# Where the running maximum lives, who masks the diagonal score blocks, and when the summing transfers leave: one change to a hybrid attention block on one Trainium2 core

## The chip, the cores and the metric

The program runs on one core of one Trainium2 chip. A core has five engines that run their own instruction streams in order and wait for each other on semaphores: TensorE (PE in the profile, with its weight loads on a second row, PEld), VectorE (DVE), ScalarE (ACT), GpSimd (POOL) and SyncE (SP), which only issues transfers. GpSimd issues some transfers too, those that add into DRAM. The metric is the device time of the program in microseconds, as a median of runs.

## The reference

The reference is a decoder block on a sequence of 1040 tokens (16 learned meta tokens before 1024 real ones) with 1024 channels. One RMS norm and one input projection feed two mixers: a causal multi-scale pooling and a forgetting attention with 8 heads of 64. Both are gated, projected up, merged with sigmoid gates, projected once more and added to the residual. Cut to the attention, which the change touches most:

```python
c = cumsum(log_sigmoid(f_logit + b_forget), axis=1)
s = einsum('bqhd,bkhd->bhqk', qb, kb) / sqrt(64)
s = s + c[:, :, q0:q1, None] - c[:, :, None, :q1]
s = where(valid, s, -inf)            # causal
p = softmax(s, axis=-1)
o = einsum('bhqk,bkhd->bqhd', p, vb)
y_attn = o * silu(z_attn)
```

## The kernel before, in words

All products run in fp32 accuracy by splitting each operand in a high part (float32r) and a low part, so that a product is three matmul groups: high by high, high by low, low by high. `whi`/`wlo`, `ph`/`pl`, `yh`/`yl`, `gw`, `gh` are such pairs. ScalarE makes the high parts, and VectorE or GpSimd subtract them from the source for the low parts.

The program has four stages: the norm and the first projections; the scores with softmax, among which the other projections are strewn; the block products that make the gates' inputs (seven products `g_prod` per result, Strassen's way); the up-projections and the last product, again by seven block products.

The score stage has 16 units: 4 head pairs `p`, 2 heads `e`, 2 halves of 512 queries. Scores stand transposed: keys on the 128 partitions, queries along the row. A unit of the first half has 5 key blocks, one of the second half 9. For a key block `b`, `Unit.qk` runs two matmuls into a PSUM bank `ps` (pool `psS`, two banks), and the result goes to SBUF as `S` with a per-key bias `negc` (the running sum of the forget gates). Where the block lies on the diagonal, its first up to 128 columns need the causal mask; `d1` is where the masked columns end and `c0` where the block begins. Before, VectorE evicted the masked columns with bias and mask in one instruction (L687), and ScalarE evicted the rest (L689), into the same tile. Then VectorE brought the running maximum `m`, an SBUF tile, up to date (L693 to L696). After the last block `Unit.maxes` reduces `m` over the keys: a 32x32 block transpose, a reduction, and two exchanges between partition groups by small ScalarE copies; the result is spread into a PSUM bank `pm`. `Unit.soft` then, block by block, subtracts `pm` (L720, VectorE), takes the exponential (L721, ScalarE), copies the high part `ph` (L724, ScalarE), subtracts for the low part `pl` (L725, VectorE), adds up the sums in `acc` (L731 and L733, GpSimd) and, two blocks later, multiplies by the values into `po` (L741). `Unit.finish` takes `po` out (L748) and stores it in two parts, `y` and `y2`, that a GpSimd transfer adds in DRAM (`add_y`).

`merged` strings the key blocks of the next unit and the softmax steps of this one together, and `F.pull` puts matmuls of other projections (`g_proj`, L170) between them. For TensorE the order in the program is the order of execution (`manual_schedule`), and the pull lengths are fixed numbers. On the other engines a scheduler of the framework orders the instructions by its own estimates; `after` ties an instruction to stand behind another in that order without a wait, `behind` makes it wait for the other's end.

`SUMS` lists what each unit does on the side: stores and loads of blocks for the later products (`put`, on SyncE), negated blocks (`put_neg`: a ScalarE copy, two GpSimd subtractions, stores) and transfers that add one DRAM block to another (`add`, on GpSimd). They were issued after `u.finish()`, and ordered behind the last sum `accs[-1]`.

The PSUM pool `psT` has two banks and serves `pm` and, near the end, one result each of the groups `ga_` and `gb_`. At the end of the gates' stage, four pooling products `pool_mm` (L170 on `plh`, `pll`) alternate with the seventh product on the four results `ga_[0]` to `ga_[3]`; each result must have been added to `zp` (`plus_`, L982) before its next product may begin. `up_weights` loads and splits the weights of an up-projection (L1098, L1099).

Of the kernel before, what the change touches and what calls it, by code (L numbers as in the profile page):

```python
# [54 lines left out]
def tile_hybrid_block(ctx, tc, x, meta, norm_g, w_in, b_forget, pool_w, pool_scale,  # L55
# [560 lines left out]
    def add_y(p):  # L616
        d, r = [spill[n, p].rearrange("(p k) c -> p (k c)", k=2) for n in ("y", "y2")]
        after(nc.gpsimd.dma_start(d, r, accum_op=ALU.add, max_dma_last_dim=8192), accs[-1])
# [26 lines left out]
    class Unit:  # L645
# [19 lines left out]
        def qk(self, b):  # L665
            p, e, q0, t0, kb, c0 = self.p, self.e, self.q0, self.t0, self.kb[b], self.c0[b]
            h = 2 * p + e
            ka, qa, ql = KA[p, e], QA[p, e], QL[p, e]
            d1 = max(0, min(512, b * KB + KB - t0))
            own_keys = b == NB - 1  # L670
            if b == 0:
                self.m = ap_.tile([KB, 512], F32, name="m")
            m = self.m
            if b % 2 == 0:
                self.st = ap_.tile([KB, 2, 512], F32, name="S", tag="s", bufs=6)
            s = self.st[:, b % 2, :]
            self.S.append(s)
            ps = psS.tile([128, 512], F32, name="ps")
            k0 = KS[b]
            nc.tensor.matmul(ps[:kb, c0:], ka[:, k0:k0 + kb], qa[:, q0 + c0:q0 + 512], start=True, stop=False)  # L680
            nc.tensor.matmul(ps[:kb, c0:], ka[:, k0:k0 + kb], ql[:, q0 + c0:q0 + 512], start=False, stop=True)  # L681
            nb_ = negc[:kb, b, h:h + 1]
            f0 = max(d1, c0)
            if d1 > c0:
                j = t0 + c0 - b * KB
                mk = tail if own_keys else mask[:, j:j + d1 - c0]
                nc.vector.scalar_tensor_tensor(s[:kb, c0:d1], ps[:kb, c0:d1], nb_, mk, op0=ALU.add, op1=ALU.add)  # L687
            if f0 < 512:
                nc.scalar.activation(s[:kb, f0:], ps[:kb, f0:], AF.Identity, bias=nb_)  # L689
            S0 = self.S[0]  # L690
            if b == 1:
                if c0:
                    nc.vector.tensor_copy(m[:, :c0], S0[:, :c0])  # L693
                nc.vector.tensor_tensor(m[:, c0:], S0[:, c0:], s[:, c0:], op=ALU.max)
            elif b > 1:
                nc.vector.tensor_tensor(m[:kb, c0:], m[:kb, c0:], s[:kb, c0:], op=ALU.max)  # L696

        def maxes(self, extra=0.0):
# [45 lines left out]
        def finish(self):  # L744
# [3 lines left out]
            nc.scalar.activation(t, po, AF.Copy)  # L748
            for n, part in (("y", hr), ("y2", lr)):
# [246 lines left out]
    add_y(3)  # L996
# [350 lines left out]
```

## Time and profile before

| | |
|---|---|
| median of 3 runs | 745.23 us (744.98 to 746.96) |
| the profiled execution's own time | 744.3 us |
| its span from first to last instruction | 742.6 us |
| TensorE busy | 720.2 us (97%) |
| VectorE, ScalarE, GpSimd busy | 536.5, 417.0, 334.4 us |
| mean granted TensorE clock | 0.996 |

An engine is busy while an instruction of it runs. Groups of instructions are named by line, engine, operation, output<-input and the shapes; after the bar stand their busy time, the mean of one in ns, the idle time of the engine just before them, and what ended it. A row of waits reads: engine, tile and line that waited, the engine and line that ended the wait, microseconds in total, times, longest. PEclk is the clock that TensorE was granted, as a share of full speed.

### The profile page before, as it was taken

How to read it: one execution, taken by the hardware profiler on the slowest of the kernel's cores; microseconds unless marked ns; L12 is line 12 of the kernel's file. 1: busy time of each engine (PE TensorE's matmuls, PEld its weight loads, DVE VectorE, ACT ScalarE, POOL GpSimd, SP SyncE). 2: the span in 40 equal slices, each digit the busy share in tenths (PEclk: the TensorE clock that was granted, in tenths of full speed). 3: DMA queues.
4: the chain of work that ended last, by engine and by line, in shares of the span. 5: the costliest groups of instructions: out<-in, count | busy, mean ns of one | idle time of the engine just before them, and what ended most of it. 6: DMA issues, size and time to landing. Idle time of an engine off the chain costs nothing.

```text
span 742.6 us, 10841 instructions
## 1 busy us (share of the span) xinstructions
PE 720.2 (97%) x3637; PEld 616.6 (83%) x3637; DVE 536.5 (72%) x917; ACT 417.0 (56%) x914; POOL 334.4 (45%) x410
## 2 busy tenths in 40 slices
PE   8999999999999899999999999999989999999996
PEld 6997989997888797898988878888868888888885
DVE  4743577777889687887877858875876554887775
ACT  6752567565675666576765566342764432626445
POOL 4412245658336584365543766473843001005243
PEclk9999999999999999999999999999999999999999
DMA  9301125897864975738475586495905457672006
GB/s 285 77 26 32 29 67 194 206 330 170 221 194 92 237 202 161 192 68 208 124 173 120 134 214 229 117 342 174 307 16 170 143 184 258 222 266 76 0 1 227
DMA packets 88906, 120.45 MB, mean 162 GB/s; under 512 B 11377, under 2 KB 54385, under 8 KB 86786
## 3 DMA queue, kind: packets, MB, share of 16 engines
q1 hardware_dynamic: 85216, 100.36, 43.0%
q0 software_dynamic: 2336, 16.78, 12.2%
q10 hardware_dynamic: 1298, 2.63, 0.9%
q8 instruction: 28, 0.46, 0.3%
q14 instruction: 28, 0.23, 0.1%
HBM read 93.33 MB, written 54.72 MB: 199 GB/s over the span
## 4 chain that ended last, share of the span: by engine, by line
PE 71%; DVE 9%; ACT 8%; issue 4%; DMA 1%; POOL 0%; POOLq 0%; DVEq 0%; ACTq 0%; SPq 0%
PE pj L170 45%; PE pj L1227 8%; PE pj L967 6%; PE po L741 4%; PE pt L1227 2%; DVE pl L725 2%; PE pt L967 2%; PE ps L680 2%; ACT S L689 2%; PE ps L681 2%; ACT S L721 1%; ACT ph L724 1%; PE pj L515 1%; DVE m L696 1%; ACT whi L156 1%
## 5 line engine op out<-in xcount | busy, mean ns | idle before, releaser
L170 PE MATMUL pj<-hh,whi 128*128 128x512 f32 (+3 forms) x640 | 145.6, 354 | 0.0
L170 PE MATMUL pj<-hh,wlo 128*128 128x512 f32 (+3 forms) x640 | 143.6, 351 | 0.0
L170 PE MATMUL pj<-hl,whi 128*128 128x512 f32 (+3 forms) x640 | 142.7, 352 | 0.0
L158 POOL TENSOR_TENSOR wlo<-raw,whi 128x256 fp32r<-128x256 f32 x116 | 91.7, 871 | 97.9 <-ACT whi L156 41.5
L170 PEld LDWEIGHTS pj<-hl,whi 128*128 128x128 f32 x640 | 108.9, 190 | 12.0
L170 PEld LDWEIGHTS pj<-hh,whi 128*128 128x128 f32 x640 | 108.8, 190 | 11.8
L170 PEld LDWEIGHTS pj<-hh,wlo 128*128 128x128 f32 x640 | 108.6, 190 | 11.5
L725 DVE TENSOR_TENSOR pl<-S,ph 128x512 fp32r<-128x512 f32 (+4 forms) x112 | 89.3, 811 | 21.2 <-ACT ph L724 20.8
L733 POOL TENSOR_TENSOR acc<-acc,S 128x272 f32<-128x272 f32 (+4 forms) x80 | 76.7, 959 | 12.5 <-ACT S L721 6.6
L689 ACT ACTIVATE S<-ps,negc 128x400 f32<-128x400 f32 (+2 forms) x96 | 48.7, 515 | 47.9 <-DVE S L687 44.4
L696 DVE TENSOR_TENSOR m<-m,S 128x272 f32<-128x272 f32 (+4 forms) x80 | 47.6, 595 | 21.1 <-ACT S L689 18.9
L721 ACT ACTIVATE S<-S 128x512 f32<-128x512 f32 (+4 forms) x112 | 49.3, 478 | 17.2 <-DVE S L720 17.0
L724 ACT ACTIVATE ph<-S 128x512 fp32r<-128x512 f32 (+4 forms) x112 | 52.3, 479 | 7.2 <-PE po L741 6.9
L136 POOL TENSOR_TENSOR gw<-graw,gw 128x256 fp32r<-128x256 f32 x40 | 44.3, 1187 | 23.5 <-ACT gw L947 14.6
L720 DVE TENSOR_TENSOR S<-S,pt 128x512 f32<-128x512 f32 (+4 forms) x112 | 50.7, 498 | 0.6
L967 PE MATMUL pj<-gh,gw 128*128 128x512 f32 x180 | 43.7, 400 | 2.6 <-DVE zp L982 2.6
L680 PE MATMUL ps<-qa,ka 128*128 128x512 f32 (+4 forms) x112 | 37.6, 335 | 7.7 <-ACT S L689 7.5
L1120 DVE TENSOR_TENSOR rl<-pj,rl 128x512 f32<-128x512 f32 x32 | 22.0, 690 | 30.3 <-PE pj L170 30.2
L967 PEld LDWEIGHTS pj<-gh,gw 128*128 128x128 f32 x180 | 34.9, 194 | 10.5 <-issue 3.0
L156 ACT ACTIVATE whi<-raw 128x512 fp32r<-128x512 f32 x58 | 33.9, 622 | 12.6 <-PE pj L170 6.2
L741 PE MATMUL po<-pl,V 128*128 128x512 f32 (+4 forms) x112 | 38.1, 340 | 2.9 <-DVE pl L725 2.6
L731 POOL TENSOR_TENSOR acc<-S 128x400 f32<-128x400 f32 (+1 forms) x16 | 20.0, 1250 | 41.5 <-ACT S L721 41.4
(228 smaller groups left out, 1345.1 us busy)
## 6 DMA issues: line engine op xcount, KB each, us to landing
raw<-in_w_in_dram SPq DMA_DIRECT2D x31, 512.0 KB, 5.9
gs<-in_w_in_dram SPq DMA_DIRECT2D x5, 1024.0 KB, 6.9
td<-in_w_out_dram SPq DMA_DIRECT2D x5, 1024.0 KB, 10.6
xt<-in_x_dram SPq DMA_DIRECT2D x8, 512.0 KB, 7.8
sp_y<-t SPq DMA_DIRECT2D x32, 128.0 KB, 2.6
gs<-gs POOLq DMA_DIRECT2D x4, 1024.0 KB, 8.7
sp_gp<-st SPq DMA_DIRECT2D x16, 256.0 KB, 4.7
td<-td POOLq DMA_DIRECT2D x4, 1024.0 KB, 8.4
```

What stands on the lines that cost most here:

```text
L158: ins = nc.gpsimd.tensor_tensor(lo[:, k:k + 2], raw[:, k:k + 2], r32(hi[:, k:k + 2]), op=ALU.subtract)
L170: nc.tensor.matmul(ps, a, b, start=(i == 0), stop=(i == len(seq) - 1))
L680: nc.tensor.matmul(ps[:kb, c0:], ka[:, k0:k0 + kb], qa[:, q0 + c0:q0 + 512], start=True, stop=False)
L689: nc.scalar.activation(s[:kb, f0:], ps[:kb, f0:], AF.Identity, bias=nb_)
L696: nc.vector.tensor_tensor(m[:kb, c0:], m[:kb, c0:], s[:kb, c0:], op=ALU.max)
L721: exps.append(nc.scalar.activation(s[:kb, c0:], s[:kb, c0:], AF.Exp))
L724: nc.scalar.activation(ph[:kb, c0:], s[:kb, c0:], AF.Copy)
L725: dves.append(nc.vector.tensor_tensor(pl[:kb, c0:], s[:kb, c0:], r32(ph[:kb, c0:]), op=ALU.subtract))
L733: accs.append(nc.gpsimd.tensor_tensor(acc[:kb, c0:], acc[:kb, c0:], s[:kb, c0:], op=ALU.add))
L741: nc.tensor.matmul(self.po[:, c0:], v, r[:kb, c0:], start=(b == 0 and i == 0), stop=(b == self.nb - 1 and i == 1))
L967: nc.tensor.matmul(ps, op_w[n][p][k // 2][:, k % 2, i * 128:(i + 1) * 128], op_h[n][q][k // 2][:, k % 2], start=start and m == 0, stop=m = ...
L1227: nc.tensor.matmul(ps, pick(A_, k, p)[:, i * 128:(i + 1) * 128], pick(B_, k, q)[:, c0:c1], start=start and n == 0, stop=n == 11, skip_grou ...
```

## The change

It has four parts.

1. The running maximum `m` becomes a PSUM bank of `psT`. The first block is copied into it by ScalarE (`AF.Copy`); every later block is folded in by one VectorE maximum with one operand in PSUM and one in SBUF. The small results `r` and `r2` of the reduction use columns of the same bank.
2. ScalarE evicts every score block whole, from `c0` to 512, with the bias. On diagonal blocks VectorE then adds the mask to the SBUF tile.
3. `sums_of` and `add_y` are called from a hook inside `maxes`, right behind the transpose of the next unit's maximum, and the adding transfers wait for that transpose (`behind ... trs[-1]`) where before they were ordered behind the last sum.
4. For the last head pair `finish` adds the two parts of `po` on the chip (a ScalarE copy of one half, a VectorE addition of the other) and stores one part; `add_y(3)` goes. At the end of the gates' stage the seventh products run in the order 3, 2, 1, 0 like the pooling products, and the first `up_weights` stands behind the last `plus_`.

```diff
     def add(dst, src):
         d, r = [t.rearrange("(p k) c -> p (k c)", k=4) for t in (dst, src)]
-        after(nc.gpsimd.dma_start(d, r, accum_op=ALU.add, max_dma_last_dim=8192), accs[-1])
+        behind(nc.gpsimd.dma_start(d, r, accum_op=ALU.add, max_dma_last_dim=8192), trs[-1])
...
             if b == 0:
-                self.m = ap_.tile([KB, 512], F32, name="m")
+                self.m = psT.tile([KB, 512], F32, name="pt")
...
             nb_ = negc[:kb, b, h:h + 1]
-            f0 = max(d1, c0)
+            nc.scalar.activation(s[:kb, c0:], ps[:kb, c0:], AF.Identity, bias=nb_)
             if d1 > c0:
                 j = t0 + c0 - b * KB
                 mk = tail if own_keys else mask[:, j:j + d1 - c0]
-                nc.vector.scalar_tensor_tensor(s[:kb, c0:d1], ps[:kb, c0:d1], nb_, mk, op0=ALU.add, op1=ALU.add)
-            if f0 < 512:
-                nc.scalar.activation(s[:kb, f0:], ps[:kb, f0:], AF.Identity, bias=nb_)
+                nc.vector.tensor_tensor(s[:kb, c0:d1], s[:kb, c0:d1], mk, op=ALU.add)
             S0 = self.S[0]
-            if b == 1:
-                if c0:
-                    nc.vector.tensor_copy(m[:, :c0], S0[:, :c0])
-                nc.vector.tensor_tensor(m[:, c0:], S0[:, c0:], s[:, c0:], op=ALU.max)
-            elif b > 1:
+            if b == 0:
+                nc.scalar.activation(m, S0, AF.Copy)
+            else:
                 nc.vector.tensor_tensor(m[:kb, c0:], m[:kb, c0:], s[:kb, c0:], op=ALU.max)
...
-            nc.vector.transpose(mt, self.m)
-            r, x, r2, y, mx = [sm.tile([128, 16], F32, name=n) for n in ("mr", "mx", "ms", "my", "mz")]
+            tr = nc.vector.transpose(mt, self.m)
+            if hook is not None:
+                hook(tr)
+            r, r2 = self.m[:, :16], self.m[:, 16:32]
+            x, y, mx = [sm.tile([128, 16], F32, name=n) for n in ("mx", "my", "mz")]
...
-            nc.scalar.activation(t, po, AF.Copy)
-            for n, part in (("y", hr), ("y2", lr)):
+            if self.p == 3:
+                nc.scalar.activation(t[hr], po[lr], AF.Copy)
+                nc.vector.tensor_tensor(t[hr], po[hr], t[hr], op=ALU.add)
+            else:
+                nc.scalar.activation(t, po, AF.Copy)
+            for n, part in (("y", hr), ("y2", lr))[:1 if self.p == 3 else 2]:
...
+    def sums_at(i, tr):
+        trs.append(tr)
+        sums_of(i)
+        if i % 4 == 1 and i > 1:
+            add_y(i // 4 - 1)
...
-            nxt.maxes()
+            nxt.maxes(hook=lambda tr: sums_at(i, tr))
         u.finish()
-        sums_of(i)
-        if i % 4 == 1 and i > 1:
-            add_y(i // 4 - 1)
...
-    add_y(3)
...
-    ws[0, 0] = up_weights(0, 0)
     plus_(zp[0][:, T1_], ga_[0])
     silu(zp[0][:, T1_], zp[0][:, T1_], -1.0)
-    for i in range(4):
-        pool_mm(3 - i)
+    ws[0, 0] = up_weights(0, 0)
+    for n, i in enumerate((3, 2, 1, 0)):
+        pool_mm(i)
         g_prod(ga_[i], 6, i, False)
-        if i:
-            silu(za[i - 1][:, T1_], ga_[i - 1])
-        if i < 2:
-            rows_[i, 0] = gate_row(i, 0)
-    silu(za[3][:, T1_], ga_[3])
+        if n:
+            silu(za[i + 1][:, T1_], ga_[i + 1])
+        if n < 2:
+            rows_[n, 0] = gate_row(n, 0)
+    silu(za[0][:, T1_], ga_[0])
```

TensorE's order is the same in both programs but for the last place below; the line numbers of the changed program are its own. The order on the other engines moves at three places that matter.

The first place is ScalarE at the start of a second-half unit (here the sixth unit), where the key blocks of this unit are evicted between the softmax steps of the unit before. `whi` are weights of a coming projection, `st` a result on its way to DRAM, `qa` queries. Before:

```order
L721 ACTIVATE S<-S 128x16
L156 ACTIVATE whi<-raw 128x512 x2
L689 ACTIVATE S<-ps,negc 128x512
L342 ACTIVATE st<-pj 128x512
L689 ACTIVATE S<-ps,negc 128x512 x3
L689 ACTIVATE S<-ps,negc 128x400
```

And now:

```order
L722 ACTIVATE S<-S 128x16
L156 ACTIVATE whi<-raw 128x512 x2
L685 ACTIVATE S<-ps,negc 128x512
L692 ACTIVATE pt<-S 128x512
L342 ACTIVATE st<-pj 128x512
L685 ACTIVATE S<-ps,negc 128x512 x4
```

The copy into the maximum's bank (L692) stands between the first and the second eviction, and the fifth block, a diagonal one, is evicted whole. On VectorE the same unit stood like this before:

```order
L694 TENSOR_TENSOR m<-S 128x512
L696 TENSOR_TENSOR m<-m,S 128x512 x2
L687 SCALAR_TENSOR_TENSOR S<-ps,negc,mask 128x112
L696 TENSOR_TENSOR m<-m,S 128x512
L725 TENSOR_TENSOR pl<-S,ph 128x144
L261 SCALAR_TENSOR_TENSOR ql<-pj,qa 64x512
L687 SCALAR_TENSOR_TENSOR S<-ps,negc,mask 128x128 x2
```

And now:

```order
L694 TENSOR_TENSOR pt<-pt,S 128x512 x3
L689 TENSOR_TENSOR S<-S,mask 128x112
L694 TENSOR_TENSOR pt<-pt,S 128x512
L726 TENSOR_TENSOR pl<-S,ph 128x144
L261 SCALAR_TENSOR_TENSOR ql<-pj,qa 64x512
L689 TENSOR_TENSOR S<-S,mask 128x128
L694 TENSOR_TENSOR pt<-pt,S 128x400
```

Each mask now stands between the block's eviction and its maximum, and reads and writes SBUF alone.

The second place is GpSimd at the end of the seventh unit, with one adding transfer (`td`), four subtractions for weights (`wlo`) and two for a negated block (`neg`). Before:

```order
L733 TENSOR_TENSOR acc<-acc,S 128x16
L590 DMA td_776<-td_780 128x2048
L158 TENSOR_TENSOR wlo<-raw,whi 128x256 x4
L604 TENSOR_TENSOR neg<-neg,hl_122 128x256 x2
L158 TENSOR_TENSOR wlo<-raw,whi 128x256 x4
L234 MEMSET ql 64x1024 x2
```

And now:

```order
L734 TENSOR_TENSOR acc<-acc,S 128x16
L158 TENSOR_TENSOR wlo<-raw,whi 128x256 x2
L606 TENSOR_TENSOR neg<-neg,hl_122 128x256 x2
L158 TENSOR_TENSOR wlo<-raw,whi 128x256 x4
L590 DMA td_776<-td_780 128x2048
L234 MEMSET ql 64x1024 x2
```

The transfer went from the head of this group to its end.

The third place is TensorE at the end of the gates' stage, where the first of the four last products follows the first pooling product. Before:

```order
L170 MATMUL pj<-plh,pwh 128x512
L170 MATMUL pj<-pll,pwh 128x512
L170 MATMUL pj<-plh,pwl 128x512
L967 MATMUL pj<-gh,gw 128x512 x12
L170 MATMUL pj<-plh,pwh 128x512
```

And now:

```order
L170 MATMUL pj<-plh,pwh 128x512
L170 MATMUL pj<-pll,pwh 128x512
L170 MATMUL pj<-plh,pwl 128x512
L975 MATMUL pt<-gh,gw 128x512 x12
L170 MATMUL pj<-plh,pwh 128x512
```

The result that is written first is now the one in the `pt` bank, `ga_[3]`; `ga_[0]`, in a `pj` bank, comes last.

More of the change, by code (lines that the diff above doesn't have):

```diff
@@ L589, in add @@
         d, r = [t.rearrange("(p k) c -> p (k c)", k=4) for t in (dst, src)]
-        after(nc.gpsimd.dma_start(d, r, accum_op=ALU.add, max_dma_last_dim=8192), accs[-1])
+        behind(nc.gpsimd.dma_start(d, r, accum_op=ALU.add, max_dma_last_dim=8192), trs[-1])
+    trs = []
     def put_h(n):
@@ L617, in add_y @@
         d, r = [spill[n, p].rearrange("(p k) c -> p (k c)", k=2) for n in ("y", "y2")]
-        after(nc.gpsimd.dma_start(d, r, accum_op=ALU.add, max_dma_last_dim=8192), accs[-1])
+        behind(nc.gpsimd.dma_start(d, r, accum_op=ALU.add, max_dma_last_dim=8192), trs[-1])
     SUMS = {
@@ L686, in qk, with maxes @@
                 mk = tail if own_keys else mask[:, j:j + d1 - c0]
-                nc.vector.scalar_tensor_tensor(s[:kb, c0:d1], ps[:kb, c0:d1], nb_, mk, op0=ALU.add, op1=ALU.add)
-            if f0 < 512:
-                nc.scalar.activation(s[:kb, f0:], ps[:kb, f0:], AF.Identity, bias=nb_)
+                nc.vector.tensor_tensor(s[:kb, c0:d1], s[:kb, c0:d1], mk, op=ALU.add)
             S0 = self.S[0]
-            if b == 1:
-                if c0:
-                    nc.vector.tensor_copy(m[:, :c0], S0[:, :c0])
-                nc.vector.tensor_tensor(m[:, c0:], S0[:, c0:], s[:, c0:], op=ALU.max)
-            elif b > 1:
+            if b == 0:
+                nc.scalar.activation(m, S0, AF.Copy)
+            else:
                 nc.vector.tensor_tensor(m[:kb, c0:], m[:kb, c0:], s[:kb, c0:], op=ALU.max)
-        def maxes(self, extra=0.0):
+        def maxes(self, extra=0.0, hook=None):
             F.pull(LM1 + extra)
             mt = ap_.tile([KB, 512], F32, name="mt")
-            nc.vector.transpose(mt, self.m)
-            r, x, r2, y, mx = [sm.tile([128, 16], F32, name=n) for n in ("mr", "mx", "ms", "my", "mz")]
+            tr = nc.vector.transpose(mt, self.m)
[3 more added lines that the diff above has]
+            x, y, mx = [sm.tile([128, 16], F32, name=n) for n in ("mx", "my", "mz")]
             nc.vector.tensor_reduce(r, mt.rearrange("p (j b) -> p j b", b=32), axis=AX.X, op=ALU.max)
```

## The prediction

> **What bounds the kernel now.** I read the page's head first, then the stages in windows, then TensorE's waits.
>
> ```profile
> PE 720.2 (97%) x3637; PEld 616.6 (83%) x3637; DVE 536.5 (72%) x917; ACT 417.0 (56%) x914; POOL 334.4 (45%) x410
> 66.00:486.00 420.00, 409.42 (x2111) 356.88 (x2110) 327.07 (x618) 257.64 (x634) 226.58 (x266) 1.00 0.63 166
> 572.00:660.00 88.00, 88.00 (x389) 72.85 (x389) 56.13 (x84) 36.33 (x50) 5.76 (x8) 1.00 0.65 219
> ```
>
> The columns of a window are its length, then busy time of PE, PEld, DVE, ACT and POOL with counts, PEclk, DMA share and GB/s. TensorE is the bound, and the change takes no matmul away. So only time in which TensorE waits or runs slowly can be won. In the score stage (66 to 486) it is idle for 420 - 409.4 = 10.6 us. From 572 to 660 it never is: what is won before is kept there. Its waits:
>
> ```profile
> PE ps L680 <- ACT S L689: 7.5, 11, 1.9
> PE po L741 <- DVE pl L725: 2.6, 3, 1.5
> PE pj L967 <- DVE zp L982: 2.6, 1, 2.6
> PEld ps L680 <- ACT S L689: 13.2, 18, 2.4
> PEld po L741 <- DVE pl L725: 4.8, 7, 1.7
> ACT S L689 <- DVE S L687: 44.4, 34, 5.4
> ```
>
> The first two make up the stage's 10.1 us. The weight load of the same matmul waits longer (13.2 and 4.8), because the matmul before still drains; so 10.1 to 18.0 us is the ceiling for all edits in the score stage. The last row says that ScalarE's evictions stand behind VectorE's masked ones for 44.4 us, and TensorE waits for evictions.
>
> **The end of the gates' stage.** One stall costs twice:
>
> ```profile
> 552.73 0.40 PE L170 MATMUL pj<-plh,pwl 128*128 128x512 f32 x1
> 555.72 4.58 PE L967 MATMUL pj<-gh,gw 128*128 128x512 f32 x12 [2.60 <-DVE zp L982]
> 569.93 2.74 PE pt L967 x12
> 247.00:251.00 4.00, 2.06 (x10) 1.35 (x9) 1.60 (x1) 2.84 (x5) 3.82 (x6) 1.00 0.94 216
> 555.00:557.00 2.00, 1.28 (x3) 1.10 (x4) 1.90 (x3) 1.33 (x3) 0.02 (x1) 0.70 0.00 0
> 557.00:560.00 3.00, 3.00 (x10) 2.30 (x9) 0.00 (x0) 0.56 (x1) 2.79 (x4) 0.63 0.00 0
> 560.00:563.00 3.00, 3.00 (x15) 2.43 (x14) 1.44 (x2) 1.12 (x2) 0.46 (x1) 1.00 0.54 175
> ```
>
> TensorE waits 2.60 us for VectorE's last addition to `zp[0]`, since the first product writes into `ga_[0]`. Then the clock is granted at 0.70 and 0.63 in the next two windows, and these twelve matmuls take 4.58 us where the same twelve later take 2.74 (the chain's row): 1.84 more. In the new order the first product writes `ga_[3]`, whose addition is long done, so TensorE goes straight on and the clock should hold: **-2.60 - 1.84 = -4.4 us**. The first `up_weights`, now behind the addition, is wanted only after four products and three pooling products more (about 15 us). The bounds: -5.0 (the start distance instead of the idle time) to 0, if something else is late there.
>
> [...]
>
> **The maximum in PSUM.** VectorE's groups, by shape where it matters:
>
> ```profile
> L696 DVE TENSOR_TENSOR m<-m,S 128x272 f32<-128x272 f32 (+4 forms) x80 | 47.6, 595 | 21.1 <-ACT S L689 18.9
> L694 DVE TENSOR_TENSOR m<-S 128x512 f32<-128x512 f32 x8 | 13.5, 1684 | 13.8 <-ACT S L689 13.8
> L694 DVE TENSOR_TENSOR m<-S 128x400 f32<-128x400 f32 x8 | 6.5, 808 | 3.5 <-ACT S L689 3.5
> L720 DVE TENSOR_TENSOR S<-S,pt 128x512 f32<-128x512 f32 x48 | 31.2, 681 | 0.6
> L720 DVE TENSOR_TENSOR S<-S,pt 128x512 f32<-128x512 f32 (+4 forms) x112 | 50.7, 498 | 0.6
> L725 DVE TENSOR_TENSOR pl<-S,ph 128x512 fp32r<-128x512 f32 x48 | 52.7, 1110 | 18.0 <-ACT ph L724 17.8
> ```
>
> The same width takes 681 ns with one operand in PSUM, but 1684 or 1110 with both in SBUF. What the extra is shows where it is longest:
>
> ```profile
> 197.21 3.07 POOL L158 TENSOR_TENSOR wlo<-raw,whi 128x256 fp32r<-128x256 f32 x4
> 197.62 3.22 DVE L694 TENSOR_TENSOR m<-S 128x512 f32<-128x512 f32 x1 [1.20 <-ACT S L689]
> 202.77 0.59 ACT L689 ACTIVATE S<-ps,negc 128x400 f32<-128x400 f32 x1 [3.19 <-DVE S L687]
> 206.69 0.33 PE L680 MATMUL ps<-qa,ka 128*128 128x144 f32 x1 [1.34 <-ACT S L689]
> 179.64 4.17 DVE L696 TENSOR_TENSOR m<-m,S 128x272 f32<-128x272 f32 x1 [0.45 <-ACT S L689]
> 184.21 0.39 PE L741 MATMUL po<-pl,V 128*128 128x272 f32 x1 [1.45 <-DVE pl L725]
> ...
> 232.26 0.28 PE L680 MATMUL ps<-qa,ka 128*128 128x16 f32 x1 [0.27 <-ACT S L689]
> 446.93 0.34 PE L680 MATMUL ps<-qa,ka 128*128 128x144 f32 x1 [0.39 <-ACT S L689]
> 280.45 0.50 PE L741 MATMUL po<-pl,V 128*128 128x512 f32 x1 [0.87 <-DVE pl L725]
> ```
>
> A maximum that starts inside a burst of GpSimd subtractions ends with the burst. Masked evictions queue behind it on VectorE, ScalarE behind them, and TensorE stops for 1.34 us; the second case stops it for 1.45. The 96 maxima have the same mix of widths as the 112 subtractions L720 less 16 full ones. So they should take 112 x 0.498 - 16 x 0.681 = 44.9 us instead of 47.6 + 13.5 + 6.5 = 67.6. That is VectorE's gain, not the kernel's. For TensorE I count the stops that I can follow to a blocked maximum or to a mask ahead of an eviction: on evictions 1.34, 0.27 and 0.39 (2.0 of the 7.5), on `po` 1.45 and the smallest of the three, 2.6 - 1.45 - 0.87 = 0.3. The 0.87 lies behind a blocked low part, which stays. **-3.7 us** (0 to -10.1).
>
> **The mask in SBUF.** Here is the other side:
>
> ```profile
> L687 DVE SCALAR_TENSOR_TENSOR S<-ps,negc,mask x72: 216/339/353, 85.6 to 448.7; 128x128 f32<-128x128 f32 x48, 128x112 f32<-128x112 f32 x16, 128x16 f32<-128x16 f32 x8
> L696 DVE TENSOR_TENSOR m<-m,S x80: 174/444/4165, 88.7 to 449.8; 128x512 f32<-128x512 f32 x24, 128x272 f32<-128x272 f32 x16, 128x144 f32<-128x144 f32 x16, 128x16 f32<-128x16 f32 x16
> L696 DVE TENSOR_TENSOR m<-m,S 128x144 f32<-128x144 f32 x16 | 5.5, 343 | 5.5 <-ACT S L689 5.5
> ```
>
> Minimum, median and maximum in ns stand behind the count. The masked eviction read PSUM and never took over 353 ns; the maximum from SBUF went up to 4165. The 80 mask additions (72 and 8 on the tail) now have both operands in SBUF, at about 343 ns each by the nearest width: no longer than before, but they can be blocked. They are fewer than the 96 maxima freed, and an eviction no longer waits for them; the end of a unit does. The blocked maxima cost TensorE 2.8 us; a third of that back, **+1.0** (0 to +2.8).
>
> [...]
>
> **ScalarE's load.** ScalarE takes over the masked columns and the copy:
>
> ```profile
> L689 ACT ACTIVATE S<-ps,negc 128x512 f32<-128x512 f32 x32 | 21.4, 682 | 3.3 <-PE ps L681 3.2
> L721 ACT ACTIVATE S<-S 128x512 f32<-128x512 f32 x48 | 28.9, 627 | 12.3 <-DVE S L720 12.2
> 248.16 0.63 ACT L602 ACTIVATE neg<-hh 128x512 f32<-128x512 f32 x1 [1.93 <-POOL wlo L158]
> 249.42 0.50 PE L680 MATMUL ps<-qa,ka 128*128 128x512 f32 x1 [1.95 <-ACT S L689]
> ```
>
> Each unit's diagonal widths (400, 272, 144, 16) move up one step to 512, 400, 272, 144, and 16 is added: as if 16 more full ones, 16 x 0.682 = 10.9 us. The copies are 16 x 0.627 = 10.0 us (a ScalarE copy of that width into PSUM isn't in the trace; this is the SBUF one). ScalarE goes from 257.6 to about 278.5 of 420 us. Mean occupancy is no danger, but place is: most of TensorE's wait on ScalarE (7.5 less the 2.0 put down to masks) is at the start of second-half units, as at 249.42, where ScalarE is late by its own queue. The copy stands just there, between first and second eviction; behind it in the queue are the later evictions, for which TensorE waits. At worst 8 x 0.63 = 5.0, at best nothing because fills cover it; half, **+2.4**.
>
> **At no cost.** The adding transfers wait for a transpose. Behind them on GpSimd stand the next unit's sums:
>
> ```profile
> POOL acc L731 <- ACT S L721: 41.4, 14, 10.5
> POOL sp_y L618 <- DVE fin L922: 9.3, 1, 9.3
> ```
>
> The sums wait 41.4 us for exponentials anyway, later than the transpose; without that cover a transfer would hold weight splits by a microsecond or two. What the order gains is that splits no longer queue behind a transfer; I price neither. SyncE's stores of a unit come in another order, four fewer; nothing reads them before the next stage. `add_y(3)` goes with its 9.3 us of GpSimd's waiting at 480, where TensorE is fed from before. Four additions of 64x512 on VectorE replace it, some 2.7 us by the 681 ns of a full width, hidden because `po` is wanted again two blocks later; if not, +2.7.
>
> **The sum** is made on the profiled execution's 744.3 us (span 742.6, 1.7 outside): -4.4 - 3.7 + 1.0 + 2.4 = -4.7, so 739.6; the median of the runs lies 0.9 above that execution, so **740.5 us** as a median, with its own range of 736 to 744.
>
> **The rivals.** *The score stage gives nearly all its waits back.* Freed of 44.4 us behind masks, ScalarE has more room than the 20.9 it takes on, and bursts find no long VectorE instruction to block. Of 10.1, 8 go: 745.2 - 4.4 - 8 = **732.8**. For it: the 44.4. Against it: the waits at unit starts have other causes.
>
> *The slow clock or the stall stays* at the end of the gates: the clock may have fallen for another cause than the gap, or another operand may be late. 1.84 to 4.4 come back: **742.3 to 744.9**. For it: a gap of 1.95 us in the window from 247 left the clock at 1.00, and splits and pooling products end close to each other here. Against it: the clock fell just at the gap's end, and the stall's releaser is the one addition. [...]
>
> *ScalarE becomes the bound of the score stage* (slower): in first-half units the copy waits for VectorE's mask on the first block, with exponentials and evictions queued behind it, and in second-half units it delays the evictions. If all 16 copies land on TensorE and nothing is won from the maxima, 745.2 - 4.4 + 10.0 = **750.8**. It decides once copies and blocked masks cost over 8.1 us, all that the other terms save. Against it: 44.4 us of ScalarE's queue go.
>
> **How the numbers follow.** The forecast has 0.55, the large gain 0.20, the stall that stays 0.15, the bound by ScalarE 0.10. What this measurement can tell from no change is about 0.3%, 2.2 us: faster is below 743.0. That is nearly all of the forecast (0.51), the large gain and a third of the stall case (0.05): 0.76. Within 0.3%: 0.04 + 0.10 = 0.14. Slower: 0.10. The range of 8 in 10 takes the forecast, most of the large gain and the stall case: 732 to 747.
>
> **What would show it.** Right: no wait of `gh,gw` on `zp` and PEclk at 1.00 through 550 to 572; no maximum above 0.75 us; no wait of an eviction on VectorE; PE waiting on ScalarE at 4 to 8 us. Wrong: mask additions of 1 to 4 us with `po` waits behind them (the mask's price), waits on ScalarE above 12 us right behind L692 (the slower rival), or TensorE idle in the score stage below 3 us (the large gain).

## The result, and the profile after

| | before | after |
|---|---|---|
| median | 745.11 us (744.41 to 746.96, 4 runs) | 737.46 us (736.24 to 738.60, 4 runs) |
| ratio | | 0.9893, 95% interval 0.9867 to 0.9919 |
| the profiled execution's own time | 744.3 us | 738.6 us |

The change gains 7.65 us by the medians. The profiled execution of the kernel after is the slowest of its four, so the two profiles lie only 5.7 us apart, and the tables below account for those. Where the time went is read best from a matmul and its twin: TensorE's order is the same up to the end of the gates, so the start of the same matmul can be compared between two traces. The table gives it for the first score matmul of a unit (by its time before), worked out from the traces; the three columns on the right are kernels of the experiments below.

| start before, us | after | sums behind the finish | two buffers | two buffers, old masks |
|---|---|---|---|---|
| 84.3 (first unit) | -1.8 | -1.9 | -0.8 | -2.0 |
| 144.6 | -3.6 | -3.8 | -2.6 | -3.8 |
| 168.9 | **+4.0** | -3.1 | -1.4 | -3.7 |
| 218.3 | +0.7 | -4.1 | -4.7 | -6.1 |
| 242.2 | +1.5 | **+1.5** | -3.8 | -6.6 |
| 293.2 | -3.4 | -2.4 | -8.6 | -11.5 |
| 316.1 | **+0.5** | -2.4 | -8.6 | -11.4 |
| 447.7 (last score matmul) | -1.5 | -3.6 | -10.6 | -13.4 |
| 735.7 (last matmul) | -6.0 | -8.1 | -13.1 | -15.9 |

The first row is not the change's: this start came 0.7 to 2.0 us earlier in every kernel that was profiled after the first, also where only the gates' end was edited. So in its profile the change won nothing net in the score stage (-1.8 at its first matmul, -1.5 at its last), and 4.4 at the end of the gates. Inside the stage it lost 7.6 us between 144.6 and 168.9 and 3.9 between 293.2 and 316.1, and won them back elsewhere. The page's first part, the windows, and TensorE's waits of the kernel after:

```profile
PE 716.8 (97%) x3637; PEld 618.4 (84%) x3637; DVE 511.0 (69%) x913; ACT 433.6 (59%) x946; POOL 325.7 (44%) x409
66.00:486.00 420.00, 408.91 (x2108) 360.39 (x2107) 306.13 (x612) 274.42 (x666) 223.08 (x266) 0.99 0.63 167
553.00:557.00 4.00, 4.00 (x19) 3.25 (x18) 3.33 (x5) 2.51 (x5) 1.70 (x3) 1.00 0.00 0
557.00:560.00 3.00, 3.00 (x15) 2.47 (x14) 2.23 (x2) 0.71 (x3) 3.00 (x4) 1.00 0.17 35
PE ps L682 <- ACT S L685: 10.0, 5, 5.9
PE po L742 <- DVE pl L726: 1.1, 1, 1.1
```

VectorE has 327.1 - 306.1 = 21.0 us less work in the score stage, ScalarE 16.8 more. The gates' end has neither wait nor slow clock. In the score stage the waits on `po` fell from 2.6 to 1.1 us, but those on ScalarE rose from 7.5 to 10.0, and one of them is 5.9 us long. The timeline there (start, length, instruction, and in brackets the idle time before it and what ended it), TensorE, ScalarE and SyncE, and the landing of the store:

```profile
145.47 0.69 PE L170 MATMUL pj<-hh,whi 128*128 128x384 f32 x3
152.05 0.80 PE L682 MATMUL ps<-qa,ka 128*128 128x512 f32 x1 [5.90 <-ACT S L685]
152.64 0.63 PE L683 MATMUL ps<-ql,ka 128*128 128x512 f32 x1
144.88 0.60 ACT L692 ACTIVATE pt<-S 128x512 f32<-128x512 f32 x1
149.76 0.63 ACT L604 ACTIVATE neg<-hh 128x512 f32<-128x512 f32 x1 [4.28 <-DMA hsA<-neg]
150.29 1.13 ACT L156 ACTIVATE whi<-raw 128x512 fp32r<-128x512 f32 x2
151.33 0.67 ACT L685 ACTIVATE S<-ps,negc 128x512 f32<-128x512 f32 x1
142.49 0.68 SPq L586 DMA_DIRECT2D hsA<-neg  x1
hsA<-neg SPq DMA_DIRECT2D x1, 256.0 KB, 7.2
```

ScalarE's copy of a negated block has one buffer, `neg`, and waits 4.28 us for the last store out of it; the next eviction stands behind it. TensorE is idle for 5.9 us, and the two matmuls after that take 0.80 and 0.63 us where the pair behind the stop at 249.42 before took 0.50 and 0.40: the granted clock is 0.50 from 149.88 to 156.71 (0.57 on average from 149 to 157 us). An adding transfer, issued at 136.76 and landed at 146.34, was in flight when the store left at 142.49. Before, the same copy stood behind two more evictions, and the store, which left 2.6 us after the adding transfer had landed, took 2.6 us:

```profile
151.49 0.63 ACT L602 ACTIVATE neg<-hh 128x512 f32<-128x512 f32 x1 [0.51 <-DMA hsA<-neg]
hsA<-neg SPq DMA_DIRECT2D x1, 256.0 KB, 2.6
```

The same happens at 294.88: TensorE waits 1.47 us for ScalarE, and ScalarE 2.93 for a store of `neg` to `hsC` that took 7.4 us where it took 2.6 before, again with an adding transfer in flight (282.32 to 292.08, the store from 286.11). A third stop, 1.68 us at 440.71, is ScalarE waiting for a load of gate weights.

### The profile page after: what moved, and what is told of

It reads as the page before. It is cut to its first block, busy times and chain, and to the rows that moved or that the text cites. A ratio compares the mean times of both kernels' runs of the same rounds, so it can differ in the third digit from the quotient of the medians.

```text
span 736.8 us, 10835 instructions
## 1 busy us (share of the span) xinstructions
PE 716.8 (97%) x3637; PEld 618.4 (84%) x3637; DVE 511.0 (69%) x913; ACT 433.6 (59%) x946; POOL 325.7 (44%) x409
## 4 chain that ended last, share of the span: by engine, by line
PE 88%; DMA 3%; DVE 1%; ACT 1%; issue 1%; SPq 0%; POOLq 0%; POOL 0%; ACTq 0%; DVEq 0%
PE pj L170 56%; PE pj L1234 8%; PE pj L975 8%; PE po L742 5%; PE pt L975 3%; PE ps L683 2%; PE ps L682 2%; PE pt L1234 2%; PE pj L515 1%; DMA hsC<-neg 1%; DMA hsA<-neg 1%; DMA graw<-in_w_in_dram 1%; ACT S L685 0%; PE pj L300 0%; DVE pl L726 0%
## 5 line engine op out<-in xcount | busy, mean ns | idle before, releaser
L170 PE MATMUL pj<-hl,whi 128*128 128x512 f32 (+3 forms) x640 | 144.2, 355 | 0.0
L158 POOL TENSOR_TENSOR wlo<-raw,whi 128x256 fp32r<-128x256 f32 x116 | 88.9, 815 | 74.7 <-PE pj L170 25.2
L170 PEld LDWEIGHTS pj<-hh,wlo 128*128 128x128 f32 x640 | 108.1, 189 | 11.4
L726 DVE TENSOR_TENSOR pl<-S,ph 128x512 fp32r<-128x512 f32 (+4 forms) x112 | 80.3, 728 | 21.1 <-ACT ph L725 19.5
L734 POOL TENSOR_TENSOR acc<-acc,S 128x272 f32<-128x272 f32 (+4 forms) x80 | 74.5, 931 | 14.6 <-ACT S L722 9.5
L685 ACT ACTIVATE S<-ps,negc 128x512 f32<-128x512 f32 (+4 forms) x112 | 59.9, 539 | 32.3 <-PE ps L683 29.8
L694 DVE TENSOR_TENSOR pt<-pt,S 128x400 f32<-128x400 f32 (+2 forms) x96 | 46.8, 487 | 34.3 <-ACT S L685 32.0
L136 POOL TENSOR_TENSOR gw<-graw,gw 128x256 fp32r<-128x256 f32 x40 | 41.7, 1075 | 37.5 <-ACT gw L955 37.5
L689 DVE TENSOR_TENSOR S<-S,mask 128x128 f32<-128x128 f32 (+2 forms) x72 | 32.9, 459 | 31.8 <-ACT S L685 31.2
L975 PE MATMUL pj<-gh,gw 128*128 128x512 f32 x180 | 42.0, 390 | 0.0
```

The source lines that it names most:

```text
L158: ins = nc.gpsimd.tensor_tensor(lo[:, k:k + 2], raw[:, k:k + 2], r32(hi[:, k:k + 2]), op=ALU.subtract)
L170: nc.tensor.matmul(ps, a, b, start=(i == 0), stop=(i == len(seq) - 1))
L685: nc.scalar.activation(s[:kb, c0:], ps[:kb, c0:], AF.Identity, bias=nb_)
L726: dves.append(nc.vector.tensor_tensor(pl[:kb, c0:], s[:kb, c0:], r32(ph[:kb, c0:]), op=ALU.subtract))
L734: accs.append(nc.gpsimd.tensor_tensor(acc[:kb, c0:], acc[:kb, c0:], s[:kb, c0:], op=ALU.add))
L975: nc.tensor.matmul(ps, op_w[n][p][k // 2][:, k % 2, i * 128:(i + 1) * 128], op_h[n][q][k // 2][:, k % 2], start=start and m == 0, stop=m = ...
```

## Experiments: the hook, the negated blocks and the adding transfers

All experiments were timed in five rounds or more, next to the kernel before. Two theories stood against each other for the 5.9 us: the hook (part 3) put the negation ahead and its store in the way of an adding transfer, or ScalarE's own load (part 2 and the copies) made it late.

**Part 3 alone**: the kernel before, `sums_of` and `add_y` called from the hook, adds behind `trs[-1]`.

> The kernel before with part 3 alone (hook, adds behind the transpose). Collision theory: the same third negated block stands ahead of an eviction, a TensorE stall of 3 to 6 us near 150 with half clock behind it, 748 to 752. Load theory: ScalarE has its old load, no such stall, 744 to 746.

Measured 751.96 us against 744.37, ratio 1.0096 (1.0071 to 1.0120). ScalarE has its old load here, and the stall is longer:

```profile
146.18 0.68 ACT L691 ACTIVATE S<-ps,negc 128x512 f32<-128x512 f32 x1
153.78 0.63 ACT L604 ACTIVATE neg<-hh 128x512 f32<-128x512 f32 x1 [6.92 <-DMA hsA<-neg]
hsA<-neg SPq DMA_DIRECT2D x1, 256.0 KB, 8.9
PE ps L682 <- ACT S L691: 15.9, 11, 7.9
```

The load theory falls: the hook makes the stall.

**Part 3 undone** in the kernel after:

```diff
-            nxt.maxes(hook=lambda tr: sums_at(i, tr))
+            nxt.maxes()
         u.finish()
+        sums_of(i)
+        if i % 4 == 1 and i > 1:
+            add_y(i // 4 - 1)
# and in add, add_y:
-        behind(nc.gpsimd.dma_start(...), trs[-1])
+        after(nc.gpsimd.dma_start(...), accs[-1])
```

> The changed kernel with its part 3 undone: all sums behind the finish, adding transfers ordered behind the last sum as before. Collision theory: no TensorE wait above 2 us in the score stage, both stalls behind negated blocks (5.90 and 1.47 us) gone, 728 to 731, so the hook cost 6 to 9 us. Load theory: 736 to 739. Third possibility (the hook itself won something that the stalls hid, by letting weight splits past the adds): slower than the kernel with late negations by 1 to 3 us.

Measured 736.73 us (736.16 to 738.64), ratio 0.9902 (0.9877 to 0.9926): not to be told from the change (0.9867 to 0.9919), though the stall is gone. The time lies in the load theory's range, but without the stalls that this theory kept; the collision theory is right on the stalls and wrong on the time. Of the third possibility the reason holds, that the hook itself wins something, and by the times about what it loses; its comparison with late negations does not (below). What comes back without it is in the waits, and on VectorE and GpSimd near 225 us:

```profile
PE po L742 <- DVE pl L726: 7.9, 4, 4.3
PE ps L682 <- ACT S L685: 2.7, 6, 1.0
224.62 0.80 POOL L590 DMA_DIRECT2D hsA<-hs  x1 [0.21 <-issue]
225.19 3.04 POOL L158 TENSOR_TENSOR wlo<-raw,whi 128x256 fp32r<-128x256 f32 x4
227.95 1.62 POOL L606 TENSOR_TENSOR neg<-neg,hl 128x256 f32<-128x256 f32 x2
224.98 4.75 DVE L689 TENSOR_TENSOR S<-S,mask 128x128 f32<-128x128 f32 x1 [1.22 <-ACT S L685]
230.89 0.58 DVE L726 TENSOR_TENSOR pl<-S,ph 128x400 fp32r<-128x400 f32 x1
```

One mask addition lasts from the issue of an adding transfer to the end of the subtractions behind it, 4.75 us, and TensorE waits 4.28 for the low part that follows. With the hook, the same run of subtractions has no issue ahead of it, and the same mask, which starts inside it too, takes 0.86 us:

```profile
229.10 1.51 POOL L606 TENSOR_TENSOR neg<-neg,hl 128x256 f32<-128x256 f32 x2
230.58 3.19 POOL L158 TENSOR_TENSOR wlo<-raw,whi 128x256 fp32r<-128x256 f32 x4
232.33 0.86 DVE L689 TENSOR_TENSOR S<-S,mask 128x128 f32<-128x128 f32 x1
```

**Adds as before, negations and stores in the hook** (the change with the second half of that diff alone):

> The changed kernel with negated blocks and plain stores in the hook as in the change, one buffer, but the adding transfers ordered behind the last sum as before, without the wait for the transpose. It fills the square of early or late adds and negations. Burst theory (a GpSimd transfer issue followed at once by a run of subtractions blocks VectorE's two-operand SBUF instructions until the run ends; without the issue ahead it does not): at least four VectorE instructions of 3 to 5 us come back and TensorE waits 4 to 8 us for pl. Collision theory (the neg store was late because an adding transfer was in flight): the wait of the third negated block shrinks from 4.3 to under 2 us. Both together 736 to 740. If the wait stays at 4 us or more, it is the two 1 MB stores behind it and not the add that make it late, and the time is 741 to 745.

Measured 743.91 us, ratio 0.9996 (0.9981 to 1.0012). Both theories of this run hold: the long VectorE instructions are back (eight above 1.85 us, up to 5.03), and the neg store, issued by the same SyncE order as in the change, lands in 2.6 us; ScalarE waits for none.

```profile
149.38 0.61 ACT L604 ACTIVATE neg<-hh 128x512 f32<-128x512 f32 x1
hsA<-neg SPq DMA_DIRECT2D x1, 256.0 KB, 2.6
PE po L742 <- DVE pl L726: 7.6, 5, 3.7
```

The time came 4 us above the range for both theories together: TensorE also waits 6.0 us for ScalarE, and half clock follows two stops, for 10.2 us in all. The two 1 MB copies still leave right behind the store, which takes 2.6 us with them all the same, so they are not what made it late; what differs from the 7.2 us in the change is the adding transfer, which left 20 us ahead of the store here.

**Adds in the hook, negations and stores behind the finish**:

```diff
-            fn(*args)
+            if (fn == add) == adds:
+                fn(*args)
# sums_of(i, True) in the hook, sums_of(i, False) behind u.finish()
```

> The changed kernel with only the adding transfers in the hook; negated blocks and plain stores are issued behind the finish in their old order among themselves. One-buffer theory: the third negated block stands behind three evictions on ScalarE again, and its store ahead of the two 1 MB stores, so its wait costs TensorE at most 2 us; bursts of splits on GpSimd stay short as in the change (no VectorE instruction of the score stage above 2 us): 728 to 733. Rival (the order of adds against stores is the trouble, wherever the copy stands): a stall of 4 us or more stays, 735 to 740.

Measured 734.82 us (734.54 to 736.68), ratio 0.9880 (0.9861 to 0.9900), between the two theories. No VectorE instruction of the score stage is above 1.85 us and the wait at 150 shrank, but ScalarE still waits 1.1 and 7.5 us for stores of `neg`, and TensorE 8.8 for ScalarE.

**Negations alone behind the finish** (the same with `fn in (n21, n12)`):

> The changed kernel, but the negated blocks (the ScalarE copy, the two GpSimd subtractions, the stores) are issued behind the finish of a unit again, and only the adds and plain stores stay in the hook. Collision theory (the hook moved the third negated block ahead of an eviction on ScalarE, and its one buffer's earlier store is late because it now leaves in the middle of an adding transfer): the 5.90 us stall at 152 and the slow clock behind it go, TensorE waits 2 to 5 us for ScalarE in the score stage instead of 10.0, and the time is 729 to 732. The stall near 294 may stay, since that copy keeps its place in ScalarE's order. Load theory (ScalarE is late because it now evicts whole blocks and makes 16 copies): the stalls stay within 1 us of where they were, 736 to 739.

Measured 751.21 us, ratio 1.0092 (1.0063 to 1.0120): a miss, 20 us off. The plain stores stayed in the hook, so on SyncE the two 1 MB copies now went ahead of the neg stores, not behind them:

```profile
142.73 1.48 SPq L586 DMA_DIRECT2D gs<-in_w_in_dram  x2
147.44 0.32 SPq L586 DMA_DIRECT2D hsA<-neg  x1
156.94 0.63 ACT L604 ACTIVATE neg<-hh 128x512 f32<-128x512 f32 x1 [7.12 <-DMA hsA<-neg]
PE ps L683 <- ACT S L686: 18.6, 7, 6.5
```

The store took 9.4 us and there are four such waits in all (7.1 and together 15.4 us on ScalarE). It confirms who waits for whom, and that moving the negation alone does not help: the single buffer has to be free, whatever the order. It also shows more than the collision theory says: the adding transfer had landed at 147.15, before this store left at 147.44, so with two plain 1 MB copies in flight (from 142.73 to 154.99) the store was no less late, 9.4 us, than with an adding transfer in the change, 7.2.

**A second buffer** for the negations, all else as in the change:

```diff
-        t = ap_.tile([128, 512], F32, name="neg")
+        t = ap_.tile([128, 512], F32, name="neg", bufs=2)
-            x, y, mx = [sm.tile([128, 16], F32, name=n) for n in ("mx", "my", "mz")]
+            x, y, mx = [sm.tile([128, 16], F32, name=n, bufs=1) for n in ("mx", "my", "mz")]
```

> The changed kernel with two buffers instead of one for the negated block (room for it comes from three small tiles of the reduction, one buffer each instead of two). Everything else, the hook included, as in the change. Theory (one-buffer theory: the stalls of 5.90 and 1.47 us, and the half clock behind each, come from the ScalarE copy that waits for the one buffer's last store, which leaves in the middle of an adding transfer): no wait of ScalarE for a store of neg, TensorE waits under 4 us for ScalarE in the score stage, 727 to 731. Rival (transfers as such are the limit: what does not wait there waits at the next load or store): 734 to 738.

Measured 730.99 us (730.15 to 732.37), ratio 0.9827 (0.9806 to 0.9848), 6.5 us below the change by the medians, and some 4.9 by the two ratios to the kernel before that ran beside each. ScalarE waits for no store of `neg`, and the score stage has no window at half clock.

```profile
PE ps L682 <- ACT S L685: 3.7, 4, 1.4
PE po L742 <- DVE pl L726: 1.1, 1, 1.1
```

## Experiments: the other parts alone

**The gates' end alone** in the kernel before:

> The kernel before with the end of the gates' stage alone in the new order. Forecast theory: the 2.60 us wait for zp and the half clock behind it (1.84 us) go together, 740.5 to 741.5. Rival (the clock falls there for another cause): only the wait goes, 742 to 743, and a PEclk under 1 stays between 555 and 560.

Measured 740.23 us against 744.37, ratio 0.9943 (0.9919 to 0.9967), so 4.1 us. Wait and slow clock went together; in this profile the clock is at full from 70 to 700 us.

```profile
553.00:557.00 4.00, 4.00 (x20) 3.24 (x18) 3.34 (x5) 2.50 (x5) 1.68 (x3) 1.00 0.00 0
```

**The maximum in PSUM alone**:

> The kernel before with the running maximum in PSUM alone (first block copied by ScalarE, one maximum per later block, small results in the same bank); masks, sums and the gates' end as before. Forecast theory: the stops behind blocked maxima (near 184, 207, 232 and 447) go, -3.7, and the copies cost 2.4: 741 to 744, no maximum above 0.75 us. Rival (the bursts of GpSimd splits stay and block the next VectorE instruction with two operands in SBUF, so the stops only change their name): 744 to 747, with pl or the copies named in TensorE's waits.

Measured 739.03 us against 743.25, ratio 0.9938 (0.9913 to 0.9962): 4.2 us, more than forecast. Both theories saw a part of it: TensorE's waits on evictions fell from 7.5 to 2.4 us, and those on low parts rose from 2.6 to 4.6, since the runs behind adding transfers now hold `pl` (up to 5.3 us). Of the stops above 0.6 us the copies are behind one, 1.08 us at 341.84, where two weight splits follow the copy on ScalarE; the longest stops of before at unit starts (1.13 at 102.44, 1.95 at 249.42) are gone, and ScalarE's order there has changed with the edit.

```profile
PE po L740 <- DVE pl L724: 4.6, 5, 2.1
PE ps L680 <- ACT S L689: 2.4, 6, 1.1
```

**Whole evictions and the mask in SBUF alone**:

> The kernel before with whole evictions by ScalarE and VectorE's mask added in SBUF alone; maximum in SBUF, sums and the gates' end as before. Forecast theory: masks are now blocked by bursts as the maxima are, +1.0 to +2.8, and ScalarE's 10.9 us more cost little: 745 to 748, with mask additions of 1 to 5 us. Rival (what counts is that evictions no longer wait 44.4 us behind VectorE): faster than before, 740 to 743, and fewer waits of TensorE for ScalarE than the 7.5 us before.

Measured 744.48 us against 743.25, ratio 1.0021 (0.9998 to 1.0043): no difference that can be told. The rival's waits did fall, and the forecast's rose by more:

```profile
PE po L739 <- DVE pl L723: 7.5, 6, 2.3
PE ps L680 <- ACT S L683: 3.3, 4, 1.3
```

**The masks as before, in the kernel with two buffers** (`scalar_tensor_tensor` from PSUM, ScalarE the rest):

> The changed kernel with two buffers for the negated blocks, but with the masked evictions on VectorE from PSUM as before. Theory (with the adds out of the way no mask is blocked for long, and whole evictions spare ScalarE its waits behind VectorE): 2 to 5 us slower than with masks in SBUF, 733 to 736, with TensorE waiting 5 us or more for ScalarE. Rival (without long blocked maxima VectorE is early enough, and ScalarE's 10.9 us less pay): 729 to 732.

Measured 729.02 us (728.52 to 730.08), ratio 0.9798 (0.9773 to 0.9823): the fastest of all, and its runs lie below those of the kernel with masks in SBUF (730.15 to 732.37), though the two did not run side by side. My theory falls, the rival holds. Evictions wait for VectorE again, but TensorE does not:

```profile
ACT S L691 <- DVE S L689: 33.0, 30, 2.0
PE ps L682 <- ACT S L691: 3.2, 5, 1.4
```

**The last head pair's finish alone**:

> The kernel before with the last head pair's finish alone: the two parts added on the chip, one part stored, no last adding transfer. Forecast: no change, within 0.3% of before. Rival (the four additions come late for po, or the missing last transfer frees the start of the gates' stage): 2 to 3 us slower or faster.

Measured 745.84 us against 744.44, ratio 1.0032 (1.0007 to 1.0057): slower by 1.4 us by the medians and by 2.4 by the ratio, with an interval of 0.5 to 4.2. In its profile the wait for `zp` at the gates' end is longer, with half clock for 6.82 us behind it instead of 3.41:

```profile
PE pj L971 <- DVE zp L986: 3.4, 1, 3.4
557.02:563.84 6.82, 5.48 (x13) 4.35 (x14) 2.51 (x4) 1.89 (x3) 2.80 (x4) 0.50 0.11 14
```

In the change that wait does not exist, so this price need not be in it. Nor is all of the profile's loss the edit's: a stop of 2.81 us at 248.39 (1.95 before), long ahead of the last head pair, has another half-clock window behind it. Why the addition to `zp` came later wasn't tried.

**Loads of the first gate weights in the hook**, on top of the second buffer (`put(g_raw0[k], ...)` moved from behind the fourteenth unit's finish):

> The changed kernel with two buffers for the negated blocks, and the two loads of the first gate weights issued in the hook of the fourteenth unit instead of behind its finish, so that ScalarE's first copy of them (it waits 2.67 us for the load near 430, with evictions behind it) finds them landed. Theory (the 1.44 us stall of TensorE near 431 is that wait): 729 to 730.5. Rival (the load only takes the place of another transfer): 731 to 733.

Measured 735.35 us (734.75 to 736.98), 4.4 slower than without: a miss. Two adding transfers leave at 415.5 and 416.1 and the loads at 416.7 instead of 423.6, right behind them, so they take 12.6 us instead of 6.8. Still they land a little sooner (the first at 428.85 instead of 429.87). The loss comes from an order that the edit did not name: with the load earlier, the scheduler also put ScalarE's copy of it earlier, ahead of the unit's first eviction. The copy waits 4.30 us where it waited 2.67, and that eviction starts at 429.83 instead of 424.81. The landing of the loads and the first eviction, without and with the move:

```profile
graw<-in_w_in_dram SPq DMA_DIRECT2D x2, 512.0 KB, 6.8
424.81 0.67 ACT L685 ACTIVATE S<-ps,negc 128x512 f32<-128x512 f32 x1
graw<-in_w_in_dram SPq DMA_DIRECT2D x2, 512.0 KB, 12.6
429.83 0.67 ACT L685 ACTIVATE S<-ps,negc 128x512 f32<-128x512 f32 x1
```

## Why the prediction was right, and where it was wrong

*The direction and the size* were right: 740.5 was forecast with 736 to 744 as its own range, 737.46 came. But the terms did not come as the sum has them, and that the total fits is in part luck: the maximum and its copy came 2.9 us better than forecast, and the zero for the hook is a loss and a gain that cancel. (Two slips of its arithmetic change nothing: the mask additions are 72, not 80, since the 8 on the tail are among the 72; and the far bound at the gates' end is -4.8 by its own rows, 2.99 and 1.84 us, not -5.0.)

*The end of the gates, -4.4*: right. Alone it measured -4.1, and in the change's trace wait and half clock are both gone. That the clock would hold was right, and so was its reading that 2.60 us of idle had been enough.

*The maximum in PSUM -3.7 and the copy on ScalarE +2.4*: together -1.3 was forecast, -4.2 measured. The copy was overpriced: alone it is behind one stop of size, 1.08 us, in the change behind one of 0.63 in the first unit. And I had left most of TensorE's waits at unit starts standing, as ScalarE's own; with nothing but the maxima changed, the longest of them went too. No maximum above 0.75 us was right (0.70 at most).

```profile
L694 DVE TENSOR_TENSOR pt<-pt,S x96: 181/516/700, 86.4 to 448.0; 128x512 f32<-128x512 f32 x32, 128x400 f32<-128x400 f32 x16, 128x272 f32<-128x272 f32 x16, 128x144 f32<-128x144 f32 x16
L689 DVE TENSOR_TENSOR S<-S,mask x72: 165/293/1390, 84.1 to 447.3; 128x128 f32<-128x128 f32 x48, 128x112 f32<-128x112 f32 x16, 128x16 f32<-128x16 f32 x8
```

*The mask in SBUF, +1.0*: of the right size. Alone it cost 1.2 us within an interval that reaches zero, and about 2.0 in the kernel with two buffers. No mask took over 1.39 us in the change, yet not for a reason that I had given: with the adding transfers behind the transpose, no VectorE instruction of the score stage is held above 1.85 us.

*Adding transfers and the order of the sums, 0*: this step failed, twice. "I price neither" stood on the sums waiting anyway. But the hook moves more than the adds. It puts the ScalarE copy of a negated block ahead of an eviction, and the store that this copy waits for into the middle of an adding transfer: 5.9 and 1.5 us of stall and the half clock behind them. The prediction looked at what the moved step issues on GpSimd and SyncE, and not at its ScalarE copy. On the other side the hook takes the long blocks of VectorE away, TensorE's 7.9 us on `po` down to 1.1. The two nearly cancel (736.73 without, 737.46 with), so the zero came out by chance.

*The last head pair's finish, 0*: alone it measured +1.4 us by the medians. Its four additions take the 2.7 us that were forecast; what it costs within the change was not measured apart.

*What would show it*: three marks were right (no wait on `zp`, short maxima, no eviction that waits for VectorE). "PE waiting on ScalarE at 4 to 8 us" was wrong: 10.0, of which 9.1 us are three waits of ScalarE for transfers that I had not listed. With the second buffer 3.7 are left.

*The rivals*: the large gain's 732.8 is close to where the change stands once the negations have a second buffer (730.99), but only half by the mechanism named there. That bursts find no long VectorE instruction to hold is borne out, by the hook's place for the adds; that ScalarE must be freed of its waits behind masks is not, since the kernel with the old masks keeps 33.0 us of them and is faster still (729.02). My reading of that, not tested apart: with no long maximum on VectorE each of these waits is short (30 of them, 2.0 us at most), and whole evictions only add work to both engines. The slow clock that stays fell with the gates' end alone (740.23), and the bound by ScalarE with TensorE's 10.0 us, of which 9.1 are waits for transfers and not for copies.

## What to carry to other kernels

When a block of side work is moved to another place in the program, list its instructions on every engine, and for each the buffer that it waits for; on ScalarE, whose evictions TensorE waits for, one late store (a wait of 4.28 us) became a stall of 5.9 us, and here a second buffer (6.5 us by the medians) was worth more than any order that was tried. In this kernel transfers that add in DRAM are better not issued ahead of a run of GpSimd arithmetic (the same mask addition took 4.75 us behind such an issue and 0.86 without), and loads or stores that someone waits for should not leave just behind 1 MB transfers, adding or plain (a store of 256 KB took 7.2 and 9.4 us there, 2.6 in the kernel before). Test the parts alone and in company: alone the five parts add up to a loss (-4.1 and -4.2, +1.2, +7.6, +1.4: +1.9 us), together they gained 7.65. The hook costs 7.6 us alone and nothing that can be told in the change, and the masks in SBUF were the one part that the best kernel does without.

## What the runs showed of the hardware

**VectorE instructions with both operands in SBUF lasted up to 5.32 us where a GpSimd transfer issue stood ahead in a run of GpSimd arithmetic.** In the fourteen profiles I counted VectorE instructions with both operands in SBUF (old maxima, low parts, mask additions) that start inside a run of GpSimd instructions without gaps above 0.15 us and with at least 2 us of it left. With a transfer issue in the run up to half a microsecond after their start, 35 of 61 took over 1.85 us, up to 5.32, and 30 of the 35 ended within 0.6 us of the run's end; with none, 0 of 802 did (1.82 at most). In the kernel before, six took 2.08 to 5.04 us (as at 179.64 and 275.36), each begun 0.2 to 1.4 us after the start of an issue; in the change, which has no issue in such a place, none took over 1.79. The place parts the 61 cleanly: all that began 0.2 to 1.8 us after the start of the last issue are the 35, and the 26 others began at most 0.1 us after it or at least 2.8. The 35 are few places of the program met again in several kernels, all of them in the seven kernels whose adding transfers are ordered behind the last sum; the kernel with the early adds (8 long instructions) and the change (none) differ in that order alone. Outside this count, the kernel with part 3 alone has two small maxima of the reduction (128x16, operands in SBUF) that start there behind an add and last 2.7 us each, and ScalarE waits up to 3.0 us for their results (1.1 before); in the change one operand of theirs is in PSUM. The prediction took the run itself for the cause; the 802 began inside a run too. Why the place of the issue matters is not shown.

**In these profiles half clock followed windows of 3.41 us in which TensorE was idle for 52% or more.** The half-clock stretches of a profile lie on a grid of 3.41 us: in the change they start at 149.88, 296.65 and 733.56, 43 and 128 times 3.413 us apart, in the kernel before at 555.78 and 740.10, 54 times. In the fourteen profiles, between 70 and 700 us, every one of the 23 windows of that grid at full clock in which TensorE was idle for 52% or more was followed by one at half clock, and none of some 2500 with 48% or less. In the kernel before, 2.60 of 3.41 us were idle from 552.37 and half clock followed; 1.54 from 245.17, and none did. In the change the clock came back to full after the windows from 153.29 and 296.65, which had no idle time, and stayed at half after the one from 149.88, with 2.17 us of it. Two windows and what followed each, of the change (idle 1.76 of 3.41) and of the kernel with the early adds (1.63):

```profile
293.24:296.65 3.41, 1.65 (x7) 0.91 (x6) 0.07 (x1) 3.00 (x6) 1.42 (x2) 1.00 1.09 356
296.65:300.06 3.41, 3.41 (x8) 2.73 (x9) 2.03 (x3) 1.17 (x2) 0.00 (x0) 0.50 0.35 103
199.08:202.49 3.41, 1.78 (x7) 0.82 (x5) 1.72 (x3) 3.38 (x8) 3.12 (x6) 1.00 1.00 286
202.49:205.91 3.42, 3.21 (x14) 2.66 (x15) 2.10 (x3) 1.51 (x4) 2.15 (x4) 1.00 1.08 204
```

So the stall of 1.47 us at 294.88 in the change cost a slow window, and the one of 1.95 us at 249.42 before, which straddles two windows (1.54 and 0.84 us idle), cost none.
